# First layer of a two-layer block: half of the weight chunks get their two parts from DMAs instead of from ScalarE, VectorE and GpSimd

## The chip, the core and the metric

The kernel runs on one core of a Trainium2 chip. The metric is the device time of one execution in microseconds (us), lower is better. The core has TensorE (PE, matmuls; PEld is its weight load), VectorE (DVE), ScalarE (ACT), GpSimd (POOL), SyncE (SP, which only issues DMAs here) and 16 DMA engines. Each engine works through its own queue in order; engines wait for each other through semaphores.

## What is computed

256 tokens of width 2048 pass through two layers. The first has chunked attention (A), an RWKV-7 scan (B) and attention to a memory (C), merged under three gates; the second has causal attention, gated linear attention, a short convolution and a feed-forward part. The part of the reference that the change touches is the first layer's projections:

```python
h = rms_norm(x, norm_g)
proj = h @ w_in                       # 2048 x 16512
(aq, ak, av, az, br, bk, bv, bz, bwd, bad, cq, cz, ga, gb, gc) = jnp.split(proj, offsets, axis=-1)
ya = chunked_band_attention(aq, ak, av, a_rel_bias) * jax.nn.silu(az)
yb = rwkv7_time_mix(br, bk, bv, bwd, bad, ...) * jax.nn.silu(bz)
mk, mv = jnp.split(rms_norm(mem, mem_norm_g) @ w_mem_kv, 2, axis=-1)
yc = memory_cross_attention(cq, mk, mv) * jax.nn.silu(cz)
merged = sigmoid(ga) * (ya @ w_up_a) + sigmoid(gb) * (yb @ w_up_b) + sigmoid(gc) * (yc @ w_up_c)
return x + merged @ w_o
```

Everything is float32. The kernel gets float32 accuracy from float32r matmuls by splitting each operand into a high part (rounded to float32r) and a low part (what the rounding lost): high*high + high*low + low*high.

## The kernel before

**Weights.** All weights come from DRAM in chunks of 128 x 1024 float32 (512 KB), 963 in all. `wchunk` (L159 to L168) makes a chunk ready: SP loads it into a buffer `w` (a pool of 4), ACT rounds it into `wh` (L163, a pool of 3), and VectorE or GpSimd subtracts to give `wl` (L167, a pool of 3). A buffer is taken again when its last reader is done: `w` after the subtraction, `wh` and `wl` after the last matmul of their chunk. So chunk n can be rounded only when TensorE is done with chunk n-3.

**Products.** `gemm_B` (L170) makes 128 features x 256 tokens out of 2 chunks of 8 k tiles: for each k tile a matmul of `wh` over 512 columns (high and low activations side by side in `xg`) and one of `wl` over 256. `gemm_A` (L182) makes 256 tokens x 512 features out of 8 chunks of 2 k tiles. `evict` (L201) adds the two halves. All matmuls and transposes are recorded at L153 and L150.

**Stages.** 0 to 134 us: memory keys and values (`w_mem`, 32 chunks). 134 to 957 us: the 206 chunks of `w1A` and `w1B` that belong to `share[0] = 0.7` (set at L334). It is the share of the low parts that GpSimd makes; with the rounding of `turn*0.7` that is 161 of the 206, and VectorE makes 45. Beside these products run the memory attention, the eight pairs of RWKV heads (`rwkv_inputs`, `rwkv_inverse`, `rwkv_chain`) and the attention A. `rwkv_inverse` lets GpSimd make `lt` and `tt` (L532, L534), `rwkv_chain` lets it make `Sd` (L608). `ahead` (L677) computes 22 gates of the merge early and puts them by in DRAM (`gdram`, a GpSimd DMA). From 957 us on `share[0]` is 0: the rest of layer one, and from 1350 us the second layer, use VectorE alone for `wl`.

**Order.** Each engine's order is fixed when the program is built: a scheduler places every instruction by its own estimate of when the inputs are ready. At the chip the engines wait in that order.

Of the kernel before, what the change touches and what calls it, by code (L numbers as in the profile page):

```python
# [8 lines left out]
F32 = mybir.dt.float32  # L9
F32R = mybir.dt.float32r  # L10
BF16 = mybir.dt.bfloat16
AF = mybir.ActivationFunctionType
ALU = mybir.AluOpType
# [13 lines left out]
# columns of the per-feature parameter tile  # L27
# [10 lines left out]
# constants that depend on shapes alone  # L38
# [7 lines left out]
# masks of zeros and ones  # L46
# [43 lines left out]
def chunks(kt):  # L90
    """k tiles of 128 in chunks of 8 or a little less."""
    n = -(-kt // 8)
    base, rem = divmod(kt, n)
    o = 0
    for i in range(n):
        s = base + (i < rem)
        yield o, s
        o += s


def _body(tc, a, out):
# [9 lines left out]
    wp = pool("w", 4)  # L111
    whp = pool("wh", 3)
    wlp = pool("wl", 3)
# [42 lines left out]
    share = [0.0]  # of the low parts, those that GpSimd makes  # L156
    turn = [0]

    def wchunk(src, nel):  # L159
        w = wp.tile([128, 1024], F32, tag="w", name="w")  # L160
        nc.sync.dma_start(w[:, :nel], src)
        wh = whp.tile([128, 1024], F32R, tag="wh", name="wh")
        nc.scalar.copy(wh[:, :nel], w[:, :nel])  # L163
        wl = wlp.tile([128, 1024], F32R, tag="wl", name="wl")
        turn[0] += 1
        eng = nc.gpsimd if turn[0] * share[0] % 1.0 < share[0] else nc.vector
        eng.tensor_sub(wl[:, :nel], w[:, :nel], wh[:, :nel].bitcast(F32))  # L167
        return wh, wl  # L168

    def gemm_B(wd, act, kt=KD, m=128):  # L170
        """[features, tokens]: both halves of the sum in one bank."""
        ps = psg.tile([128, 512], F32, tag="g", name="g")
        for k0, kn in (chunks(kt) if m == 128 else [(0, kt)]):
            src = wd[128 * k0 * m:128 * (k0 + kn) * m].rearrange("(p c) -> p c", p=128)
            wh, wl = wchunk(src, kn * m)
            for j in range(kn):
                k = k0 + j
                mm(ps[:m, :], wh[:, j * m:(j + 1) * m], act[:, k, :], start=(k == 0), stop=False)
                mm(ps[:m, 256:512], wl[:, j * m:(j + 1) * m], act[:, k, 0:256], start=False, stop=(k == kt - 1))
        return ps  # L180

    def gemm_A(wd, act, kt=KD, ahead=None):  # L182
        """[tokens, 512 features] for two token tiles."""
        ps = [psg.tile([128, 512], F32, tag="g", name="g") for _ in range(2)]
        for k0 in range(0, kt, 2):
            if ahead:
                ahead(k0)
            src = wd[128 * k0 * 512:128 * (k0 + 2) * 512].rearrange("(p c) -> p c", p=128)
            wh, wl = wchunk(src, 1024)
            for j in range(2):  # L190
                k = k0 + j
                for tt in range(2):
                    hi = act[:, k, tt * 128:(tt + 1) * 128]
                    lo = act[:, k, 256 + tt * 128:256 + (tt + 1) * 128]
                    h_ = wh[:, j * 512:(j + 1) * 512]
                    l_ = wl[:, j * 512:(j + 1) * 512]
                    mm(ps[tt], hi, h_, start=(k == 0), stop=False)
                    mm(ps[tt], hi, l_, start=False, stop=False)
                    mm(ps[tt], lo, h_, start=False, stop=(k == kt - 1))
        return ps  # L200
# [13 lines left out]
    def split_to(hl, k, src, g=None):  # L214
        """hi and lo parts of src*g into hl[:, k, 0:256 | 256:512]."""
        hi = hl[:, k, 0:256]
        if g is None:
            nc.scalar.copy(hi, src)
            nc.vector.tensor_sub(hl[:, k, 256:512], src, hi.bitcast(F32))
        else:  # L220
            nc.scalar.activation(hi, src, AF.Copy, scale=g)
            nc.vector.scalar_tensor_tensor(hl[:, k, 256:512], src, g, hi.bitcast(F32), op0=ALU.mult, op1=ALU.subtract)
# [15 lines left out]
    def rsqrt(u, y):  # L238
        """u = 1/sqrt(u), with one Newton step; y is scratch of the same shape."""
# [6 lines left out]
    def stats(acc, bc=None, col=None):  # L246
        """1/rms of the tokens: one per partition in col, along the free axis in bc."""
# [28 lines left out]
    def prepare(src, acc, split, squares):  # L276
        """Loads two k tiles at a time, ahead of their products."""
# [26 lines left out]
    if True:  # L304
# [29 lines left out]
        share[0] = 0.7  # L334
        # raw branch outputs; the last part holds token-major tiles meanwhile
# [6 lines left out]
        # sums of squares per head, then 1/sqrt for q and k together  # L342
# [70 lines left out]
        def shift(dst, z, mu):  # L413
            """z [128, 257] with a zero column first; dst = z + mu*(prev - z)."""
# [15 lines left out]
        # queries and keys of four heads of A, and one of two sets of token-major tiles  # L430
# [5 lines left out]
        # block-diagonal operands: zeros stay, the diagonal blocks are rewritten  # L436
# [20 lines left out]
        def rwkv_inputs(p):  # L457
            """Products for a pair of heads, and what the chunks need of them."""
# [26 lines left out]
            # kk normalised per head  # L485
# [9 lines left out]
            # k2 = k*(1 + (a-1)*k_a)  # L495
            nc.vector.tensor_scalar(t0, av_, -1.0, P("k_a", p), op0=ALU.add, op1=ALU.mult)
            nc.vector.scalar_tensor_tensor(k, t0, 1.0, k, op0=ALU.add, op1=ALU.mult)
            # bonus weight r*k2*r_k summed per head
# [15 lines left out]
        def rwkv_inverse(p):  # L514
            """Products inside the chunks and (I - L)^-1, two chunks at a time: doubling of blocks
            in float32r, then one Newton step on the exact L."""
# [65 lines left out]
        def rwkv_chain(p):  # L582
            """The chunks in order, then group norm, affine and bonus."""
# [35 lines left out]
            # group norm per head (over the partitions of a head)  # L619
# [14 lines left out]
        def attn128(qT, kT, v_of, finish, bias, qscale, escale):  # L634
            """Two query tiles against keys 0..127 and 0..255; qT, kT [128, 256]."""
# [27 lines left out]
        def silu2(z):  # L663
            """2*silu(z), in place."""
# [12 lines left out]
        def ahead(i):  # L677
            """A gate of the merge, before its sigmoid, put by in DRAM."""
# [34 lines left out]
        # products that do not wait for the chain of the chunks, to run beside it  # L713
# [63 lines left out]
    def residual(wd, act, kt, xres, src, gname, hl):  # L777
        """xres[:, m] = src(m) + act @ w; sums of squares; split of xres*g into hl."""
# [24 lines left out]
    # ================= second layer =================  # L803
# [10 lines left out]
    # gate inputs of the decays  # L814
# [18 lines left out]
    # r gates  # L833
# [140 lines left out]
def _layout(i):  # L974
    """Layouts of the inputs; no arithmetic on them."""
    def tiles(w, n=128):
        """Column tiles of n; in each, chunks of k tiles follow one another, [128, k, n] each."""
# [69 lines left out]
```

## Time and profile before

| | |
|---|---|
| runs | 3015.86, 3016.11, 3016.77 us (median 3016.11) |
| profiled execution, span | 3013.1 us |
| median less span (start and end around the span) | 3.0 us |
| TensorE busy in the span | 2941.7 us, 98% |
| VectorE, ScalarE, GpSimd busy | 1958.8, 1448.1, 581.4 us |
| DRAM read | 514.56 MB, 172 GB/s on average |

A row of instructions gives line, engine, operation, what it writes <- what it reads, shapes and count, then busy us in all and mean ns of one, then the idle time of the engine just before and what ended it. A row of stretches gives the stretch's length, each engine's busy us (and number of instructions), then the granted TensorE clock as a share of full speed, the mean busy share of the DMA engines, and GB/s.

### The profile page before, as it was taken

What the parts mean: (1) busy time and instruction counts of PE and PEld (TensorE: products, weight loads), DVE (VectorE), ACT (ScalarE), POOL (GpSimd) and SP (SyncE); (2) the same over time, 40 slices, a digit from 0 to 9 for tenths busy, and PEclk for the clock granted to TensorE, in tenths of its full rate; (3) what the DMA queues carried; (4) which work ended last, traced back from release to release, by engine and by line L of the source; (5) the groups of instructions that cost most, each with busy time, mean ns of one, the idle gap of its engine ahead of it and who ended that gap; (6) DMA issues with size and microseconds to landing.
All of it is one profiled execution on the core that took longest, in us unless ns stands there. A gap on an engine that the chain in (4) does not pass through costs nothing.

```text
span 3013.1 us, 43980 instructions
## 1 busy us (share of the span) xinstructions
PE 2941.7 (98%) x16704; PEld 2582.1 (86%) x16704; DVE 1958.8 (65%) x3086; ACT 1448.1 (48%) x2179; POOL 581.4 (19%) x441
## 2 busy tenths in 40 slices
PE   8998999999999999999999999999999999999998
PEld 6887888887888888888888888888888888888887
DVE  6368675677764755665766766666676666666554
ACT  5454444434445645555444444445455444444443
POOL 6455555644554100000000000000000000000000
PEclk9999999999999999999999999999999999999999
DMA  7643333433435766665445555555565555556564
GB/s 253 205 142 123 129 127 121 136 98 123 133 130 180 226 189 189 202 204 171 160 161 168 183 191 191 190 189 190 188 193 186 191 191 190 189 189 186 191 190 146
DMA packets 151252, 522.42 MB, mean 173 GB/s; under 512 B 17200, under 2 KB 22320, under 8 KB 151040
## 3 DMA queue, kind: packets, MB, share of 16 engines
q1 hardware_dynamic: 148208, 512.72, 52.6%
q0 software_dynamic: 1824, 4.98, 0.4%
q8 instruction: 131, 2.15, 0.3%
q10 hardware_dynamic: 1008, 1.90, 0.2%
q14 instruction: 81, 0.66, 0.1%
HBM read 514.56 MB, written 4.98 MB: 172 GB/s over the span
## 4 chain that ended last, share of the span: by engine, by line
PE 90%; DVE 8%; POOL 1%; ACT 1%; issue 1%; DMA 0%; SPq 0%; DVEq 0%; ACTq 0%
PE g L153 83%; PE G L153 1%; PE ch L153 1%; PE D L153 1%; PE oT L153 1%; PE sc L153 1%; PE po L153 1%; PE Z L153 1%; POOL acc L293 1%; DVE kt_d L509 0%; DVE wl L167 0%; POOL sq L289 0%; DVE bt_d L508 0%; DVE tA L416 0%; DVE tt L564 0%
## 5 line engine op out<-in xcount | busy, mean ns | idle before, releaser
L153 PE MATMUL g<-xg,wh 128*128 128x512 f32 x4640 | 1641.1, 394 | 2.3 <-DVE zr L207 2.2
L163 ACT CAST wh<-w 128x1024 fp32r<-128x1024 f32 (+1 forms) x963 | 1004.1, 1043 | 1269.7 <-PE g L153 696.9
L167 DVE TENSOR_TENSOR wl<-w,wh 128x1024 fp32r<-128x1024 f32 (+1 forms) x802 | 986.6, 1231 | 740.5 <-ACT wh L163 738.6
L153 PE MATMUL g<-xg,wl 128*128 128x256 f32 x4640 | 1325.1, 286 | 4.0 <-DVE wl L167 3.8
L153 PEld LDWEIGHTS g<-xg,wh 128*128 128x128 f32 x4640 | 874.6, 189 | 179.0 <-issue 2.6
L153 PEld LDWEIGHTS g<-xg,wl 128*128 128x128 f32 x4640 | 881.8, 190 | 6.8 <-DVE wl L167 4.2
L167 POOL TENSOR_TENSOR wl<-w,wh 128x1024 fp32r<-128x1024 f32 x161 | 391.3, 2433 | 256.6 <-ACT wh L163 235.3
L153 PE MATMUL g<-yhl,wh 128*128 128x512 f32 x768 | 271.9, 393 | 3.1 <-ACT wh L163 1.8
L153 PE MATMUL g<-wh,xg 128*128 128x512 f32 x768 | 251.3, 402 | 1.7 <-DVE z L207 1.3
L153 PE MATMUL g<-act,wh 128*128 128x512 f32 x704 | 244.1, 390 | 0.0
L153 PE MATMUL g<-yhl,wl 128*128 128x256 f32 x768 | 217.7, 284 | 0.6 <-DVE wl L167 0.6
L153 PE MATMUL g<-act,wl 128*128 128x256 f32 x704 | 198.7, 282 | 0.0
L771 POOL TENSOR_TENSOR accm<-accm,z 128x256 f32<-128x256 f32 x64 | 48.0, 751 | 661.1 <-DVE z L770 661.1
L153 PEld LDWEIGHTS g<-yhl,wh 128*128 128x128 f32 x768 | 145.3, 189 | 33.8 <-ACT wh L163 3.7
L153 PEld LDWEIGHTS g<-wh,xg 128*128 128x128 f32 x768 | 143.9, 190 | 32.8 <-DVE z L207 1.6
L204 ACT COPY et<-g 128x256 f32<-128x256 f32 (+1 forms) x434 | 157.9, 364 | 10.4 <-PE g L153 7.4
L153 PEld LDWEIGHTS g<-act,wh 128*128 128x128 f32 x704 | 132.1, 188 | 27.5
L153 PE MATMUL g<-wl,xg 128*128 128x512 f32 x384 | 154.7, 403 | 0.0
L153 PEld LDWEIGHTS g<-yhl,wl 128*128 128x128 f32 x768 | 146.5, 191 | 1.2 <-DVE wl L167 1.1
L153 PEld LDWEIGHTS g<-act,wl 128*128 128x128 f32 x704 | 133.4, 189 | 0.0
L207 DVE TENSOR_TENSOR z<-g,et 128x256 f32<-128x256 f32 x216 | 90.3, 418 | 25.1 <-ACT et L204 24.8
L153 PE MATMUL g<-wh,mem_hl 128*128 128x512 f32 x256 | 83.2, 406 | 8.1 <-ACT wh L163 8.1
(349 smaller groups left out, 2960.8 us busy)
## 6 DMA issues: line engine op xcount, KB each, us to landing
w<-w2B SPq DMA_DIRECT2D x208, 512.0 KB, 3.4
w<-w1B SPq DMA_DIRECT2D x194, 512.0 KB, 3.4
w<-w_gate SPq DMA_DIRECT2D x88, 512.0 KB, 3.5
w<-w_ffup SPq DMA_DIRECT2D x88, 512.0 KB, 3.4
w<-w1A SPq DMA_DIRECT2D x64, 512.0 KB, 3.4
w<-w_down SPq DMA_DIRECT2D x64, 448.0 KB, 3.3
w<-w_mem SPq DMA_DIRECT2D x32, 512.0 KB, 4.6
w<-w_o SPq DMA_DIRECT2D x32, 512.0 KB, 4.0
```

What stands on the lines that cost most here:

```text
L153: nc.tensor.matmul(dst, lhsT=lhsT, rhs=rhs, start=start, stop=stop)
L163: nc.scalar.copy(wh[:, :nel], w[:, :nel])
L167: eng.tensor_sub(wl[:, :nel], w[:, :nel], wh[:, :nel].bitcast(F32))
L204: nc.scalar.copy(t[:m], ps[:m, 256:512])
L207: nc.vector.tensor_add(z[:m], ps[:m, 0:256], t[:m])
L293: nc.gpsimd.tensor_add(acc, acc, s)
L771: nc.gpsimd.tensor_add(accm, accm, u)
```

## The change

While `share[0]` is above zero, every second chunk (103 of 206) takes another way. GpSimd issues a DMA that casts the float32 chunk from DRAM straight into `wh`; ACT writes the negative of `wh` into `wl`; GpSimd issues a second DMA that reads the chunk from DRAM again and adds it onto `wl`. The other 103 chunks go as before, with the subtraction always on VectorE; GpSimd makes none. The pool `w` has 3 buffers instead of 4 and `wl` has 4 instead of 3, for the whole kernel. Comments that were dropped move the line numbers by about four.

```diff
-    wp = pool("w", 4)
+    wp = pool("w", 3)
     whp = pool("wh", 3)
-    wlp = pool("wl", 3)
+    wlp = pool("wl", 4)
...
     def wchunk(src, nel):
+        wh = whp.tile([128, 1024], F32R, tag="wh", name="wh")
+        wl = wlp.tile([128, 1024], F32R, tag="wl", name="wl")
+        turn[0] += 1
+        if turn[0] * share[0] % 1.0 < share[0]:
+            nc.gpsimd.dma_start(wh[:, :nel], src)
+            nc.scalar.mul(wl[:, :nel], wh[:, :nel].bitcast(F32), -1.0)
+            nc.gpsimd.dma_start(wl[:, :nel], src, accum_op=ALU.add)
+            return wh, wl
         w = wp.tile([128, 1024], F32, tag="w", name="w")
         nc.sync.dma_start(w[:, :nel], src)
-        wh = whp.tile([128, 1024], F32R, tag="wh", name="wh")
         nc.scalar.copy(wh[:, :nel], w[:, :nel])
-        wl = wlp.tile([128, 1024], F32R, tag="wl", name="wl")
-        turn[0] += 1
-        eng = nc.gpsimd if turn[0] * share[0] % 1.0 < share[0] else nc.vector
-        eng.tensor_sub(wl[:, :nel], w[:, :nel], wh[:, :nel].bitcast(F32))
+        nc.vector.tensor_sub(wl[:, :nel], w[:, :nel], wh[:, :nel].bitcast(F32))
         return wh, wl
...
-        share[0] = 0.7
+        share[0] = 0.5
```

GpSimd's queue beside the inverse and the chain of a pair of heads, in the middle of the stage (`Sd`, `lt`, `tt` are steps of those; a name's number tells buffers apart). Before:

```order
L532 TENSOR_TENSOR lt_3712<-lt_3712,con_92 128x256
L534 TENSOR_TENSOR tt_3710<-tt_3710,con_92 128x512
L608 TENSOR_SCALAR Sd_3659<-S_3644,ep_2719 128x128
L167 TENSOR_TENSOR wl_5233<-w_5229,wh_5231 128x1024
L532 TENSOR_TENSOR lt_3735<-lt_3735,con_92 128x256
L534 TENSOR_TENSOR tt_3733<-tt_3733,con_92 128x512
L167 TENSOR_TENSOR wl_5251<-w_5247,wh_5249 128x1024
L167 TENSOR_TENSOR wl_5290<-w_5286,wh_5288 128x1024
L608 TENSOR_SCALAR Sd_3676<-S_3658,ep_2719 128x128
```

Now, at the same place of the same pair:

```order
L164 DMA wh_4624<-w1B 128x1024
L612 TENSOR_SCALAR Sd_3626<-S_3611,ep_2699 128x128
L166 DMA wl_4625<-w1B 128x1024
L536 TENSOR_TENSOR lt_3679<-lt_3679,con_92 128x256
L538 TENSOR_TENSOR tt_3677<-tt_3677,con_92 128x512
L536 TENSOR_TENSOR lt_3702<-lt_3702,con_92 128x256
L538 TENSOR_TENSOR tt_3700<-tt_3700,con_92 128x512
L164 DMA wh_4677<-w1B 128x1024
L612 TENSOR_SCALAR Sd_3643<-S_3625,ep_2699 128x128
L164 DMA wh_4776<-w1B 128x1024
L166 DMA wl_4678<-w1B 128x1024
```

The subtractions are gone; casts (L164), which wait for TensorE to free a `wh`, and accumulations (L166), which wait for ACT's negative of the same chunk, stand between the steps of the pair.

GpSimd's queue near the end of the stage, where the last gates are computed ahead. Before:

```order
L167 TENSOR_TENSOR wl_8628<-w_8624,wh_8626 128x1024
L680 DMA gdram_101<-z_8570 128x256
L167 TENSOR_TENSOR wl_8678<-w_8674,wh_8676 128x1024
L608 TENSOR_SCALAR Sd_8018<-S_8000,ep_6666 128x128
L680 DMA gdram_101<-z_8620 128x256
L167 TENSOR_TENSOR wl_8700<-w_8696,wh_8698 128x1024
L680 DMA gdram_101<-z_8670 128x256
```

Now:

```order
L164 DMA wh_8404<-w1B 128x1024
L633 TENSOR_TENSOR raw_961<-raw_961,oT_7951 128x256
L164 DMA wh_8453<-w1B 128x1024
L166 DMA wl_8405<-w1B 128x1024
L684 DMA gdram_101<-z_8378 128x256
L166 DMA wl_8454<-w1B 128x1024
L164 DMA wh_8502<-w1B 128x1024
```

The last step of the last pair (L633) now has ten casts for gates behind it; before it stood behind all of these chunks.

TensorE's queue at the boundaries of chunks there (each row is one matmul). Before, a chunk of the same tile `g` follows the other:

```order
L153 MATMUL g_8673<-xg_106,wh_8676 128x512
L153 MATMUL g_8673<-xg_106,wl_8678 128x256
L153 MATMUL g_8673<-xg_106,wh_8698 128x512
L153 MATMUL g_8673<-xg_106,wl_8700 128x256
L153 MATMUL g_8673<-xg_106,wh_8698 128x512
```

Now (`wh_8404` comes by cast, `wh_8431` by SP):

```order
L153 MATMUL g_8332<-xg_106,wh_8355 128x512
L153 MATMUL g_8332<-xg_106,wl_8356 128x256
L153 MATMUL g_8381<-xg_106,wh_8404 128x512
L153 MATMUL g_8430<-xg_106,wh_8431 128x512
L153 MATMUL g_8430<-xg_106,wl_8432 128x256
```

TensorE does the first matmul of the cast chunk, leaves it, works through the SP chunk of the next tile, and comes back to the cast chunk's `wl` after that.

## Rows read from the trace of the kernel before

**Rows 1.** The page: span, and each engine's busy time.

```profile
span 3013.1 us, 43980 instructions
PE 2941.7 (98%) x16704; PEld 2582.1 (86%) x16704; DVE 1958.8 (65%) x3086; ACT 1448.1 (48%) x2179; POOL 581.4 (19%) x441
```

**Rows 2.** Stretches of the span: busy us by engine, clock, DMA share, GB/s.

```profile
134.00:180.00 46.00, 43.87 (x225) 36.41 (x223) 24.28 (x34) 25.52 (x33) 29.11 (x14) 1.00 0.52 164
180.00:900.00 720.00, 681.23 (x3991) 599.33 (x3992) 505.23 (x952) 313.38 (x482) 384.51 (x246) 0.97 0.38 125
900.00:957.00 57.00, 57.00 (x345) 50.91 (x344) 19.75 (x31) 25.52 (x38) 38.45 (x25) 1.00 0.59 184
957.00:1350.00 393.00, 389.31 (x2208) 343.26 (x2208) 255.48 (x374) 213.30 (x350) 35.15 (x53) 0.99 0.63 201
```

**Rows 3.** Stretches around a pause of TensorE, same columns as rows 2.

```profile
281.00:286.00 5.00, 1.21 (x7) 0.64 (x5) 4.91 (x7) 2.09 (x4) 2.83 (x3) 0.96 0.38 131
286.00:292.40 6.40, 4.51 (x14) 3.87 (x15) 5.93 (x12) 0.63 (x1) 2.81 (x4) 0.50 0.26 82
```

**Rows 4.** Timeline in a full-rate stretch: start us, us, engine, line, instruction.

```profile
919.62 0.39 PE L153 MATMUL g<-xg,wh 128*128 128x512 f32 x1
919.97 0.40 PE L153 MATMUL g<-xg,wh 128*128 128x512 f32 x1
920.45 1.05 ACT L163 CAST wh<-w 128x1024 fp32r<-128x1024 f32 x1 [1.73 <-issue]
921.59 2.40 POOL L167 TENSOR_TENSOR wl<-w,wh 128x1024 fp32r<-128x1024 f32 x1 [0.69 <-ACT wh L163]
```

**Rows 5.** Groups by line and form, 134 to 957 us.

```profile
L167 POOL TENSOR_TENSOR wl<-w,wh 128x1024 fp32r<-128x1024 f32 x153 | 372.1, 2435 | 232.7 <-ACT wh L163 211.4 <-issue 9.7 <-PE tra L150 7.2
L163 ACT CAST wh<-w 128x1024 fp32r<-128x1024 f32 x196 | 205.3, 1047 | 269.2 <-PE g L153 190.8 <-issue 65.4 <-POOL wl L167 5.0
L667 DVE SCALAR_TENSOR_TENSOR z<-et,z 128x256 f32<-128x256 f32 x24 | 20.7, 864 | 4.3 <-ACT et L666 4.3
L416 DVE TENSOR_TENSOR tA<-zr 128x256 f32<-128x256 f32 x25 | 19.3, 771 | 0.9 <-DVE zr L207 0.5
L242 DVE TENSOR_TENSOR t<-t,tA 128x256 f32<-128x256 f32 x8 | 10.2, 1280 | 0.1
L536 ACT CAST lmr<-lt 128x256 fp32r<-128x256 f32 x16 | 6.5, 406 | 27.6 <-POOL lt L532 27.6
L680 POOL DMA_DIRECT2D gdram<-z x20 | 11.7, 585 | 9.2 <-DVE U L598 2.9 <-DVE z L207 2.9 <-DVE mx L645 1.9
```

**Rows 6.** Groups by line and form, 1000 to 3000 us, where GpSimd makes no `wl`.

```profile
L167 DVE TENSOR_TENSOR wl<-w,wh 128x1024 fp32r<-128x1024 f32 x646 | 792.7, 1227 | 586.8 <-ACT wh L163 586.3
L242 DVE TENSOR_TENSOR osq<-osq,nw 128x256 f32<-128x256 f32 x4 | 1.7, 420 | 0.1
```

**Rows 7.** DMA issues: issuing queue, count, KB each, median us from issue to landing.

```profile
w<-w1A SPq DMA_DIRECT2D x64, 512.0 KB, 3.4
w<-wuc SPq DMA_DIRECT2D x16, 512.0 KB, 4.3
gdram<-z POOLq DMA_DIRECT2D x22, 128.0 KB, 3.9
xin<-xT POOLq DMA_DIRECT2D x16, 128.0 KB, 3.5
bias<-relb SPq DMA_DIRECT2D x8, 128.0 KB, 2.6
```

**Rows 8.** Timeline at the end of the stage: split of the raw branches for the merge.

```profile
955.38 7.17 ACT L218 CAST yhl<-raw 128x256 fp32r<-128x256 f32 x23
957.61 7.79 DVE L219 TENSOR_TENSOR yhl<-raw,yhl 128x256 fp32r<-128x256 f32 x23
```

**Rows 9.** Timeline in the second layer: a `w` buffer from subtraction to next load.

```profile
2504.29 1.23 DVE L167 TENSOR_TENSOR wl<-w,wh 128x1024 fp32r<-128x1024 f32 x1 [1.22 <-ACT wh L163]
2505.54 3.10 SPq L161 DMA_DIRECT2D w<-w_gate  x2
2505.97 1.05 ACT L163 CAST wh<-w 128x1024 fp32r<-128x1024 f32 x1 [1.46 <-issue]
2508.75 1.05 ACT L163 CAST wh<-w 128x1024 fp32r<-128x1024 f32 x1 [1.41 <-issue]
```

## The prediction

> **What bounds the kernel now.** First the page's busy times, to see which engine has no air: TensorE is busy 98% of the 3013.1 us span, VectorE 65%, ScalarE 48%, GpSimd 19% [rows 1]. Then the stretches, to see where the air is. In the stage that the change touches, 134 to 957 us, TensorE is busy 43.9 of 46, 681.2 of 720 and 57 of 57 us [rows 2]: 41 us idle in 823. The clock there is 0.97 of full over 720 us, so about 43 us run at half speed (1.2 instead of 2.4 GHz) and lose half of that, 22 us. What comes before such a spell is seen in one place: TensorE is busy 1.2 of 5.0 us while VectorE works 4.9 of the 5, then the clock is 0.50 for 6.4 us [rows 3]. Third, a timeline of a full-rate stretch: one k tile (a `wh` and a `wl` matmul) takes 0.35 us, a chunk of eight 2.8 us; ACT rounds a chunk in 1.05 us, GpSimd starts its subtraction 0.1 us later and needs 2.40 [rows 4]. From the moment TensorE frees a `wh`, then, a new chunk is ready in some 3.6 us, against the two chunks (5.6 us) that TensorE still has. That is why it can run without a gap although `wh` has only three buffers: the load itself is ahead of that loop, in `w`. So TensorE sets the end, the weight loop is hidden with 2 us to spare, and the idle time comes from the steps of the RWKV pairs.
>
> **What can be gained.** GpSimd's subtractions go: 372 us in the stage [rows 5]. They delay VectorE. The same step (L242, 128 x 256) takes 1.28 us in this stage and 0.42 where GpSimd makes no `wl` [rows 5, 6]; L416 takes 0.77 and L667 0.86 for the same amount of data. These three groups alone carry 8 x 0.86 + 25 x 0.35 + 24 x 0.44 = 26 us, and most two-operand steps of a pair are of this kind; I take 100 us for all, an estimate from these factors. The Trainium skill ("SBUF — State Buffer", Who interferes with whom) says that a VectorE instruction with two SBUF inputs and a GpSimd instruction that reads SBUF block each other for a whole instruction; the L242 pair of rows agrees. VectorE gets 103 - 45 = 58 more subtractions at 1.23 us [rows 6], 71 us. Its load thus falls by about 30 us, but the 71 us are work that can fill its pauses, and the 100 us lie in chains that TensorE waits for. The most that this can give is what TensorE loses now: 41 + 22 us, and 7 to 8 us behind 957 us, where 23 roundings and 23 subtractions of `yhl` stand in one row before the merge can start (7.2 and 7.8 us [rows 8], 3.7 idle and a clock of 0.99 over 393 us [rows 2]). These steps now start before the last ten casts. I take 30 of these 71 us: the pairs also wait for TensorE and ACT, which get no faster.
>
> **What the new way costs: its length.** A cast chunk has no `w` ahead of the loop. Cast, negative and accumulation all lie between freed `wh` and first use of `wl`. The rows of before show no cast and no accumulation, so each is bounded by plain loads. From 128 to 512 KB a load on SP's queue grows from 2.6 to 3.4 us; GpSimd's queue needs 3.5 for 128 KB [rows 7], so 4.3 for a chunk; where the DMA engines are busy 0.63 instead of 0.38 [rows 2], loads take 4.3 instead of 3.4, which would make it 5.2. The change adds 103 reads of 0.5 MB, so I take 4.6. The negative: 1.05 us, as the rounding of the same size [rows 5], and 0.6 of waiting in ACT's queue. The accumulation must read `wl` too: 512 KB more at 0.8 us per 384 KB, 1.1, so 5.7, and 0.5 for GpSimd's queue. Four hand-overs of 0.1 [rows 4]. Sum L = 4.6 + 1.05 + 0.6 + 5.7 + 0.5 + 0.4 = 12.9, say **13 us**. Lower end: 4.3 + 1.05 + 4.3 = 9.7, an accumulation at the price of a plain load and no queue. Upper end: nothing here excludes that the DMA engines convert or add at half their rate and both transfers double their moving part; with busy DMA engines 6.5 + 1 + 1 + 8 + 0.5 = 17 us.
>
> **What covers it.** I counted in TensorE's new order what stands between the matmul that frees the buffer and the first use of `wl`, at 0.35 us per k tile and 0.2 to 0.3 us per small matmul. In the first eight cast chunks (`w1A`, nothing beside them) it is two chunks and a little, 6.4 us on average. In the last sixteen it is 9.7: TensorE takes an SP chunk of the next tile first. In the 79 between, where steps of the pairs stand too, it is 13, from 8.7 to 18.8. The shortfall of one chunk overlaps with that of the next cast chunk, whose buffer is already free while TensorE waits; so half of it counts. At L = 13: 8 x 6.6 / 2 = 26; 16 x 3.3 / 2 = 26; of the 79, those below 13 lack 68 us together, half is 34. Sum **86 us**. At 9.7 it is 13 + 5 + 2 = 20, at 17 it is 42 + 58 + 161 = 261.
>
> **Queues.** GpSimd's queue holds an accumulation until ACT's negative is there, some 6 us after its cast, and behind it stand `lt`, `tt`, `Sd` and the `gdram` stores. ACT waits for `lt` already now, 27.6 us in all [rows 5]; ACT in turn stands at a negative until the cast has landed, with evictions and roundings behind it. If a third of the 64 `lt`, `tt` and `Sd` steps come 1 us later for the chain of a pair, that is 21 us: I take 20, from 0 (the scheduler put them where they fit) to 60. The 206 issues themselves take 0.585 us each [rows 5], 120 us of GpSimd instead of 372: hidden. SP loses 103 loads, ACT's count of 206 operations stays: nothing. A rule that speaks against the change: the skill's same page (SBUF: two separate sides) warns that GpSimd cannot write descriptors while VectorE holds the shared port in a two-port mode. The 0.585 us of an issue in this stage are the nearest row; at that price the rule adds nothing to the sum, and no run here shows it under accumulations.
>
> **Three `w` buffers.** In the second layer a buffer freed by the subtraction at 2504.3 is loaded from 2505.5; roundings follow at 2506.0 and 2508.7 [rows 9], 2.78 us apart. With four buffers that load is needed at the fourth, 2514.3, 4.4 to 5.4 us after it landed (3.4 to 4.3 us [rows 7]); with three at 2511.5, still 1.7 us or more ahead. Hidden, except in pile-ups and in the start, which waits for loads: 5 us, from 0 to 15. The fourth `wl` costs nothing.
>
> **Sum.** Span 3013.1 + 86 + 20 + 5 - 30 = 3094; the median of the runs lies 3.0 us over the span, so 3097, and I say **3095 us**.
>
> **Rivals.** (1) The new way is hidden and VectorE's relief shows. It decides at L of about 10 us: at 9.7 the stalls are 20 us, and if the queues cost nothing, 30 to 45 us of gain leave 2990 to 3006. For it speaks the factor of three on VectorE's steps; against it GpSimd's 3.5 us for a quarter of a chunk. The Trainium skill ("DMA: Bandwidth & Descriptors", Anatomy of one DMA) gives 2.0 us plus bytes / 436 GB/s for a GpSimd DMA, 3.2 us for a chunk; by that estimate L would be about 9 and this rival would win. The trace does not agree: the same formula gives 2.3 us for 128 KB where the row shows 3.5 [rows 7]. (2) A slow DMA path, L of 17 us or more: 3016 + 261 + 40 - 30 = 3287, and more if pauses of 4 to 5 us bring the half clock of rows 3 again and again. For it: nothing of before shows a cast or an add; against it: a plain load moves its last 384 KB in 0.8 us, so the DMA engines are far from the bound. (3) Both sides cancel, L near 10.7: stalls of about 30 us against 30, 3010 to 3022. (4) The scheduler lets the order absorb the casts elsewhere, so that the change does not do what it says to TensorE; its new order shows the covers counted above, so this is part of (1).
>
> **How the numbers follow.** Forecast, 3022 to 3200 with L from 11 to 14.5: 0.58. Rival 1: 0.20. Rival 2: 0.13. Rival 3: 0.09. A measurement of this kernel tells about 0.2%, 6 us, from no change. Faster by more than that 0.20, within it 0.09, slower 0.71. The range runs from 2988, the near end of rival 1, to 3290, where rival 2 begins; that leaves out some 0.15.
>
> **What will show it.** Right: accumulations (L166) land 5 us or more after issue; TensorE's idle time in the stage grows from 41 to over 100 us and is ended by DMAs into `wl`; the first `w1A` chunks and the last gates lose most per chunk; L242 falls from 1.28 to about 0.45 us; from 957 us on nothing changes but the `yhl` pause. Wrong: landings of 3.5 us, or a TensorE that loses its time to `lt`, `Sd` or ACT instead.

## The result, and the profile after

| | before | after |
|---|---|---|
| runs, us | 3015.86 to 3016.77 (4), median 3016.00 | 3183.21 to 3204.77 (4), median 3193.23 |
| profiled execution, span | 3013.1 | 3203.0 |
| TensorE idle in the span | 71.4 | 194.5 |
| time at the half clock | 47.8, in 9 spells | 184.3, in 37 spells |
| first load for the merge (`wuc`) issued | 946.0 | 1116.6 |

The changed kernel is slower: 1.059 times the time of before, 95% interval 1.056 to 1.062. That is 177 us more, where 79 were forecast. The direction was right and the time lies in the range, but the size was missed by more than half.

Idle time is the span less TensorE's busy time. Time at the half clock is the sum of the stretches of the trace with a granted clock of 0.50 of full (1.2 instead of 2.4 GHz), without the last one of each kernel, which lies at the end of its span. Half of it is lost where TensorE works, and nothing more where it stands, since that time is idle time already. TensorE works in 153.9 of the 184.3 us, and in 43.1 of the 47.8. So between the two profiled executions its idle time grew by 123 us and the loss by the half clock by (153.9 - 43.1) / 2 = 55 us: 178 of the 190 us that the span grew. The other 12 us are in TensorE's busy time, and no run here says what they are. (The profiled execution of after is the longest of its four; the table of all runs below goes by profiled executions and their spans.)

The page of after: span, busy times, the row of the granted clock, and two of the new transfers (KB each, median us from issue to landing).

```profile
span 3203.0 us, 43972 instructions
PE 3008.5 (94%) x16704; PEld 2619.9 (82%) x16704; DVE 1922.2 (60%) x3144; ACT 1444.3 (45%) x2176; POOL 345.3 (11%) x486
PEclk9889899899999899999999999999999999999999
wh<-w1B POOLq DMA_DIRECT2D x71, 512.0 KB, 5.3
wl<-w1B POOLq DMA_DIRECT2D x71, 512.0 KB, 5.5
```

Against [rows 1], VectorE and GpSimd are busy for less time and TensorE for more, though its matmuls are the same 16704: of the 67 us more, 55 are the half clock. The clock row is below 9 in five of the first 14 slices (to 1121 us) and in none behind them.

Stretches of after; columns as in [rows 2]. The stage now ends at 1147 us instead of 957.

```profile
100.00:200.00 100.00, 71.51 (x272) 55.45 (x271) 17.93 (x19) 26.81 (x31) 13.50 (x19) 0.85 0.62 156
200.00:1000.00 800.00, 700.64 (x3894) 607.47 (x3893) 464.86 (x1002) 305.47 (x473) 187.49 (x276) 0.93 0.62 158
1000.00:1147.00 147.00, 114.85 (x560) 95.13 (x559) 46.59 (x85) 53.04 (x84) 28.87 (x43) 0.88 0.73 179
1147.00:1545.00 398.00, 391.24 (x2221) 343.85 (x2220) 248.97 (x351) 207.02 (x330) 42.29 (x53) 1.00 0.61 200
```

TensorE is idle 28.5, 99.4 and 32.1 us in the three parts of the stage. It works for 19.5, 98.7 and 29.0 us of them at the half clock, which costs half of that: 10, 49 and 15 us. Behind 1147 us it is idle 6.8 us at full clock, against 3.7 at 0.99 in the same work of before [rows 2], and from there to the end both kernels take 2056 us: nothing is lost there, and the 7 to 8 us that the prediction saw before the merge are not won.

The timeline of the first of these pauses in after: start us, us, engine, line, instruction, and in brackets the idle time before it and what ended it.

```profile
113.31 1.06 ACT L165 ACTIVATE wl<-wh 128x1024 fp32r<-128x1024 f32 x1 [0.84 <-DMA wh<-w1A]
113.92 0.54 POOL L164 DMA_DIRECT2D wh<-w1A  x1 [4.89 <-PE g L153]
114.67 0.90 POOL L166 DMA_DIRECT2D wl<-w1A  x1 [0.21 <-issue]
119.75 1.06 ACT L165 ACTIVATE wl<-wh 128x1024 fp32r<-128x1024 f32 x1 [5.38 <-DMA wh<-w1A]
121.11 0.87 POOL L166 DMA_DIRECT2D wl<-w1A  x1 [5.54 <-ACT wl L165]
122.24 0.80 PE L153 MATMUL g<-wl,xg 128*128 128x512 f32 x1 [8.16 <-DMA wl<-w1A]
```

The chain can be read off: a cast has landed at 113.3, the negative is there at 114.4, the accumulation goes out at 114.7 and TensorE gets its `wl` at 122.2, after 8.2 us of standing. In that time the next cast chunk has gone through its cast (113.9 to 119.7) and its negative. This is the overlap that the prediction counted on.

Stretches of after around this pause, same columns as above: the pause, the work until the next one, and the spell at the half clock by itself.

```profile
113.60:122.30 8.70, 0.54 (x4) 0.10 (x2) 0.13 (x1) 1.83 (x2) 2.31 (x3) 0.71 0.75 181
122.30:135.60 13.30, 13.30 (x47) 10.60 (x48) 2.45 (x2) 2.49 (x3) 0.55 (x1) 0.80 0.49 118
117.31:127.55 10.24, 5.31 (x13) 4.15 (x14) 0.00 (x0) 1.65 (x2) 0.87 (x1) 0.50 0.66 123
```

After the pause the clock is 0.80 over 13.3 us. The `wh` matmuls behind it stand 0.43 us apart and not 0.23 for some 5 us, then at full rate. It is the pattern of [rows 3], and it comes with each of the first four pauses: the clock stands at 0.50 from 117.3, 141.2, 161.7 and 182.2 us on, for 6.8 to 10.2 us. Each of these spells begins while TensorE still stands; 3.7 to 5.5 us of each fall on its work.

Waits of after from 134 to 1150 us: who waited for what, us in total, times, longest.

```profile
POOL wl L166 <- ACT wl L165: 376.6, 73, 12.7
ACT wl L165 <- DMA wh<-w1B: 198.6, 61, 8.0
PE g L153 <- DMA wl<-w1B: 66.5, 41, 4.6
PEld g L153 <- DMA wl<-w1A: 56.1, 18, 7.9
PE g L153 <- ACT wh L170: 10.5, 9, 2.0
PE g L153 <- DVE wl L171: 7.6, 10, 1.6
```

Most of TensorE's idle time is ended by accumulations, as forecast: 126 of 160 us. GpSimd and ACT stand for the two steps ahead of them.

Groups of after by line and form, 134 to 1150 us, columns as in [rows 5]. Lines are four higher than before: L246 was L242, L420 was L416, L671 was L667, L540 was L536.

```profile
L420 DVE TENSOR_TENSOR tA<-zr 128x256 f32<-128x256 f32 x25 | 12.6, 504 | 0.3
L671 DVE SCALAR_TENSOR_TENSOR z<-et,z 128x256 f32<-128x256 f32 x24 | 10.1, 422 | 8.1 <-ACT et L670 8.0
L540 ACT CAST lmr<-lt 128x256 fp32r<-128x256 f32 x16 | 6.4, 400 | 15.9 <-POOL lt L536 15.9
L246 DVE TENSOR_TENSOR t<-t,tA 128x256 f32<-128x256 f32 x8 | 3.3, 415 | 0.0
```

VectorE's relief came as said: L242 from 1280 to 415 ns, L667 from 864 to 422, L416 from 771 to 504 [rows 5]. The Trainium skill ("SBUF — State Buffer", Who interferes with whom) has a VectorE instruction with two SBUF inputs and a GpSimd instruction that reads SBUF block each other; these rows agree. And ACT's wait for `lt` fell from 27.6 to 15.9 us, so no loss shows there from the transfers in GpSimd's queue.

The issues of the accumulations in after: duration of one in ns (least, median, most), and the time to landing.

```profile
L166 POOL DMA_DIRECT2D wl<-w1B x71: 847/872/953, 198.8 to 1145.2; - x71
L166 POOL DMA_DIRECT2D wl<-w1A x32: 852/870/914, 114.7 to 836.5; - x32
DMA to landing us min/median/max: 5.1/5.5/9.7
```

Matched chunk by chunk in the trace, the means of the 103 chains are: cast 5.65 us to its landing, 0.41 until ACT begins, negative 1.06, 0.47 until GpSimd issues, accumulation 6.21. Together **13.8 us**; the forecast had 12.9, rounded to 13.

The same matching gives what TensorE does between the issue of a cast and the first use of its `wl`, in us at the full clock: 6.0 on average in the first eight cast chunks, 11.3 in the middle (7.9 to 15.3), 10.0 in the last sixteen. By this count the shortfalls, each chain less its own cover, are 55, 205 and 69 us.

Casts also stand in GpSimd's queue. Here a cast comes out directly behind an accumulation that stood for its negative:

```profile
1017.25 0.86 POOL L166 DMA_DIRECT2D wl<-w1B  x1 [5.19 <-ACT wl L165]
1017.95 0.73 POOL L164 DMA_DIRECT2D wh<-w1B  x1
```

So it is with 21 of the 103 casts, and the accumulations before them had stood 114.7 us in all; 5 of the 16 `Sd` and 2 of the 16 `lt` stand like this too.

### The profile page after: what moved, and what is told of

It reads as the page before. It is cut to its first block, busy times and chain, and to the rows that moved or that the text cites. A ratio compares the mean times of both kernels' runs of the same rounds, so it can differ in the third digit from the quotient of the medians.

```text
span 3203.0 us, 43972 instructions
## 1 busy us (share of the span) xinstructions
PE 3008.5 (94%) x16704; PEld 2619.9 (82%) x16704; DVE 1922.2 (60%) x3144; ACT 1444.3 (45%) x2176; POOL 345.3 (11%) x486
## 3 DMA queue, kind: packets, MB, share of 16 engines
HBM read 568.56 MB, written 4.98 MB: 179 GB/s over the span
## 4 chain that ended last, share of the span: by engine, by line
PE 63%; DMA 2%; issue 2%; POOL 1%; DVE 1%; ACT 0%; DVEq 0%; POOLq 0%; SPq 0%; ACTq 0%
PE g L153 62%; DMA wl<-w1B 1%; DMA zs<-gdram 1%; DMA wh<-w1B 0%; PE glo L153 0%; POOL accm L775 0%; DVE xr L972 0%; POOL wl L166 0%; PE sc L153 0%; PE po L153 0%; PE kv L153 0%; ACT wh L170 0%; POOL wh L164 0%; POOL gdram L684 0%; PE gln L153 0%
## 5 line engine op out<-in xcount | busy, mean ns | idle before, releaser
L153 PE MATMUL g<-xg,wh 128*128 128x512 f32 x4640 | 1659.8, 398 | 19.1 <-ACT wh L170 10.5
L171 DVE TENSOR_TENSOR wl<-w,wh 128x1024 fp32r<-128x1024 f32 (+1 forms) x860 | 1054.4, 1226 | 932.5 <-ACT wh L170 931.1
L170 ACT CAST wh<-w 128x1024 fp32r<-128x1024 f32 (+1 forms) x860 | 896.0, 1042 | 1187.8 <-PE g L153 709.5
L153 PEld LDWEIGHTS g<-xg,wh 128*128 128x128 f32 x4640 | 883.3, 191 | 205.0 <-ACT wh L170 13.3
L153 PE MATMUL g<-wh,xg 128*128 128x512 f32 x768 | 272.4, 430 | 0.4 <-ACT va L322 0.4
L165 ACT ACTIVATE wl<-wh 128x1024 fp32r<-128x1024 f32 x103 | 109.1, 1059 | 270.6 <-DMA wh<-w1B 198.6
L153 PE MATMUL g<-wl,xg 128*128 128x512 f32 x384 | 170.8, 445 | 61.0 <-DMA wl<-w1A 59.8
L153 PEld LDWEIGHTS g<-wh,xg 128*128 128x128 f32 x768 | 158.8, 209 | 36.4 <-ACT va L322 0.5
L153 PEld LDWEIGHTS g<-wl,xg 128*128 128x128 f32 x384 | 81.1, 211 | 83.7 <-DMA wl<-w1A 64.7
```

The lines of the kernel that those rows point to most:

```text
L153: nc.tensor.matmul(dst, lhsT=lhsT, rhs=rhs, start=start, stop=stop)
L165: nc.scalar.mul(wl[:, :nel], wh[:, :nel].bitcast(F32), -1.0)
L171: nc.vector.tensor_sub(wl[:, :nel], w[:, :nel], wh[:, :nel].bitcast(F32))
```

## The experiments

Theory A in the texts is that of the prediction: each cast chunk has a chain of some 13 us against what TensorE has to do meanwhile, and only the shortfall costs. The rivals stand in the texts in their own words. The runs with VectorE alone, with a smaller share on GpSimd and with the pools alone start from the kernel before, the others from the changed one.

**VectorE alone, no transfer on GpSimd.**

```diff
-        share[0] = 0.7
+        share[0] = 0.0
```

> The kernel before with the GpSimd share at 0: VectorE makes all 206 low parts of the stage, no cast or accumulating DMA. It measures the relief alone. Theory A (the loss of the changed kernel comes from the long chain cast, negative, accumulation against three wh buffers, and the relief of VectorE is real): VectorE's contention goes (L242 from 1.28 to about 0.45 us), 161 subtractions of 1.23 us come on top, TensorE's idle time stays near 41 us in the stage; 2990 to 3030 us. Rival B (GpSimd and ACT waiting at the head of their queues is what costs, and taking work off GpSimd gives nothing or VectorE becomes the bound): 3030 us or more.

2981.72 us, ratio 0.989 (0.9875 to 0.9905). Better than expected: to take the subtractions from GpSimd and give all 206 to VectorE is itself a gain of 33 us. Groups and stretches of this kernel, 134 to 957 us and 100 to 905 us:

```profile
L167 DVE TENSOR_TENSOR wl<-w,wh 128x1024 fp32r<-128x1024 f32 x206 | 256.5, 1245 | 83.1 <-ACT wh L163 82.0
L416 DVE TENSOR_TENSOR tA<-zr 128x256 f32<-128x256 f32 x25 | 10.4, 416 | 0.1
L242 DVE TENSOR_TENSOR t<-t,tA 128x256 f32<-128x256 f32 x8 | 3.3, 418 | 0.0
...
100.00:200.00 100.00, 100.00 (x504) 84.28 (x503) 61.13 (x88) 50.01 (x63) 2.47 (x8) 1.00 0.53 184
200.00:905.00 705.00, 690.80 (x4131) 614.77 (x4130) 559.34 (x1080) 323.21 (x490) 84.33 (x121) 0.99 0.39 134
```

TensorE is idle 14.2 us in 805. VectorE has 161 more subtractions than before at 1.245 us, 200 us, and TensorE still waits less. So the casts cost not 177 us but 3193 - 2982 = **211 us**, against this kernel; the forecast had 86 + 20 + 5 = 111.

**A smaller share on GpSimd.**

```diff
-        share[0] = 0.7
+        share[0] = 0.25
```

> The kernel before with a GpSimd share of 0.25 of the low parts, between 0.78 (3014) and none (2982). If the contention of GpSimd's subtractions with VectorE is what the relief is made of, the time lies between, near 2990 to 3000 us; if VectorE's load in the run with none held it back, this one is faster than 2982.

2983.08 us, ratio 0.9896 (0.9881 to 0.9911): the same as none, where a time in between was expected. VectorE's steps do lie in between; this row is from 134 to 957 us:

```profile
L242 DVE TENSOR_TENSOR t<-t,tA 128x256 f32<-128x256 f32 x8 | 4.7, 587 | 0.0
```

So the time does not follow these steps in proportion. A subtraction of GpSimd also takes 2.4 us where VectorE needs 1.2, and no run separates what of the 33 us comes from the blocking and what from the longer way of a chunk.

**The pools alone.**

```diff
-    wp = pool("w", 4)
+    wp = pool("w", 3)
...
-    wlp = pool("wl", 3)
+    wlp = pool("wl", 4)
```

> The kernel before with only the pools changed (w 3 instead of 4, wl 4 instead of 3). All theories: 3016 to 3022 us; anything above 3030 would say that the smaller w pool carries a part of the loss, in the later stages too.

3019.04 us, ratio 1.0014 (1.0005 to 1.0024): 3 to 5 us, as forecast.

**The cast alone.** `wh` comes by the cast DMA, SP loads `w` as before, VectorE subtracts.

```diff
             nc.gpsimd.dma_start(wh[:, :nel], src)
-            nc.scalar.mul(wl[:, :nel], wh[:, :nel].bitcast(F32), -1.0)
-            nc.gpsimd.dma_start(wl[:, :nel], src, accum_op=ALU.add)
+            w = wp.tile([128, 1024], F32, tag="w", name="w")
+            nc.sync.dma_start(w[:, :nel], src)
+            nc.vector.tensor_sub(wl[:, :nel], w[:, :nel], wh[:, :nel].bitcast(F32))
             return wh, wl
```

> The changed kernel without the accumulation: half of the chunks get wh by the cast DMA, SP loads the same chunk into w beside it, and VectorE subtracts. Theory A: the chain from freed wh to wl is cast 5.6 + subtraction 1.2 + hand-overs 0.3 = 7.1 us instead of 13.8, under the cover of nearly all chunks; stalls under 15 us, half-clock time back near that of before; 2990 to 3030 us. Rival B (the GpSimd queue with its casts in front of the steps of the pairs): GpSimd still waits for freed buffers at each cast, so 3060 us or more.

3033.36 us, ratio 1.0065 (1.0048 to 1.0082): 52 us over VectorE alone, just above the expected range. Waits of this kernel, 134 to 1000 us:

```profile
ACT wh L171 <- DMA w<-w1B: 73.4, 19, 7.9
DVE wl L167 <- DMA wh<-w1B: 72.3, 40, 5.8
```

Now VectorE waits for casts, and ACT for SP's loads (three `w` buffers, each held until a cast has landed). The casts land after 4.6 us here.

**The accumulation alone.** SP loads, ACT rounds as before, then negative and accumulation.

```diff
-            nc.gpsimd.dma_start(wh[:, :nel], src)
+            w = wp.tile([128, 1024], F32, tag="w", name="w")
+            nc.sync.dma_start(w[:, :nel], src)
+            nc.scalar.copy(wh[:, :nel], w[:, :nel])
             nc.scalar.mul(wl[:, :nel], wh[:, :nel].bitcast(F32), -1.0)
             nc.gpsimd.dma_start(wl[:, :nel], src, accum_op=ALU.add)
```

> The changed kernel without the cast DMA: SP loads w, ACT rounds it into wh and writes the negative, and the accumulating DMA adds. Theory A: chain 1.05 + 1.06 + 0.3 + 0.5 + 6.2 = 9.1 us against a cover of 6.4 (first chunks), 13 and 9.7 us; stalls of about 20 us and 10 more by the clock; 3000 to 3060 us. Rival B: as in the changed kernel GpSimd waits for ACT at each accumulation, so half or more of the loss stays, 3100 us or more.

3041.48 us, ratio 1.0084 (1.0065 to 1.0102): 60 us over VectorE alone. The first row below is GpSimd's wait for the negative, the second TensorE's for accumulations, 134 to 1000 us:

```profile
POOL wl L168 <- ACT wl L167: 347.6, 73, 14.0
PE g L153 <- DMA wl<-w1B: 29.6, 21, 4.6
```

One half of the chain costs 52, the other 60, both in series 211, that is 99 more than the two together. This fits theory A: the two lengths one behind the other stand under one cover. It is no clean split, since each half brings waits of its own, as for SP's loads above. Both halves read as much from DRAM as the changed kernel, 568.56 MB, so the second reading as such is not what costs 211 us.

**Another cover.** Four `wh` and three `wl`, so that a cast can start a chunk earlier.

```diff
-    whp = pool("wh", 3)
-    wlp = pool("wl", 4)
+    whp = pool("wh", 4)
+    wlp = pool("wl", 3)
```

> The changed kernel with the pools wh 4 and wl 3 instead of wh 3 and wl 4: a cast may start one chunk earlier, the rest is the same. Theory A (the chain of 13.8 us from cast to landed accumulation, against the time in which TensorE uses up the other wh buffers): with one more buffer the cover counted in TensorE's new order rises from 12.3 to 13.6 us at the median and the shortfalls at 14 us halve, from 120 to 61 us; with the half clock some 90 us less than the changed kernel, 3080 to 3130 us. Theory C (GpSimd's queue in series: cast, landing 5.65, negative 1.06, accumulation issued, and only then the next cast; 8.5 us a cast chunk, 103 of them 875 us): another buffer doesn't shorten that, 3160 us or more.

3114.49 us, ratio 1.0334 (1.0316 to 1.0352), in A's range. The chain is as long as in the changed kernel (13.7 us), but the median cover, counted in TensorE's order, is 13.6 instead of 12.3 us (from the issue of the cast, in the traces, 11.9 instead of 11.0), and 79 us of the 211 are gone. If GpSimd worked off the transfers in series, a fourth `wh` would have changed little. That casts stand in its queue is not the main cost either: here 42 of them come out directly behind an accumulation, against 21.

**Half as many casts.**

```diff
-        share[0] = 0.5
+        share[0] = 0.25
```

> The changed kernel with every fourth chunk on casts (51) instead of every second (103). Theory A: each cast chunk still has to fit 13.8 us under a cover of 12 us at the median, and now no shortfall overlaps with the next one; counted in the new order 100 to 108 us of stall, with the clock 150, less 30 of VectorE's relief: 3100 to 3150 us, nearly as slow as with half. Theory C: GpSimd is busy 8.5 us for every four chunks (16 us), far from the bound: the loss all but vanishes, 2985 to 3030 us.

3060.48 us, ratio 1.0148 (1.0128 to 1.0169): under A's range and over its rival's, so both missed. With 51 casts the cost against VectorE alone is 79 us, 1.5 per cast; with 103 it is 2.0. The transfers of this kernel:

```profile
wh<-w1B POOLq DMA_DIRECT2D x35, 512.0 KB, 4.4
wl<-w1B POOLq DMA_DIRECT2D x35, 512.0 KB, 5.8
```

The cast lands after 4.4 us instead of 5.3, and the chain is 12.2 us long instead of 13.8. The accumulations are no faster than in the changed kernel; it is the casts that get slower the more is in flight (4.4 here, 4.6 with 103 casts and no accumulation, 5.3 with 103 of each). The trace of after shows it by itself: its 19 casts that no other cast or accumulation overlapped landed after 4.4 us on average, the other 84 after 5.9. And in the kernel with half as many no cast comes out directly behind an accumulation. That was in neither text.

**A longer chain.** The negative is written twice.

```diff
             nc.scalar.mul(wl[:, :nel], wh[:, :nel].bitcast(F32), -1.0)
+            nc.scalar.mul(wl[:, :nel], wh[:, :nel].bitcast(F32), -1.0)
```

> The changed kernel with the negative written twice: 1.06 us more in each chain, nothing else. Theory A: shortfalls counted in the new order at 15 instead of 14 us are 30 to 40 us more, with the clock 45 to 60: 3230 to 3260 us. Theory C: 103 times 1.06 us in series on a queue that is nearly full, about 85 to 110 us: 3270 to 3300 us.

3210.03 us, ratio 1.065 (1.0632 to 1.0668): 17 us more, less than either text. The chain is 14.8 us long, 1 us longer, but the median cover in the new order is 13.1 us instead of 12.3, and TensorE's idle time grew by 8 us only. So ACT's negative is not worked off in series with the transfers (theory C's 3270 us or more). Since the order moved too, the run does not give the price of 1 us of chain.

**No casts where nothing covers them.** The first 16 chunks of the stage go by SP.

```diff
-        if turn[0] * share[0] % 1.0 < share[0]:
+        if turn[0] > 48 and turn[0] * share[0] % 1.0 < share[0]:
```

> The changed kernel with the casts beginning at the 17th chunk of the stage: the first 16 chunks, where nothing stands between the chunks to cover a cast, all go by SP, 95 casts are left. Theory A, each stall is a local shortfall of cover and a pause brings its own half clock: what goes is the 28.5 us of idle time and half of the 30 us at half clock that 100 to 200 us hold now, 43 us: 3150, from 3135 to 3165 us. Rival B, the transfers as such are the bound and the stalls move to the next casts: 3175 us or more.

3144.02 us, ratio 1.0444 (1.0422 to 1.0466), as A said: eight casts cost 44 (by the ratios) to 49 us (by the medians). The stretch from 100 to 200 us, which had 71.51 us of TensorE and a clock of 0.85, and the first of the four copies that ACT makes of the second tile's results, when the 16 chunks are done:

```profile
100.00:200.00 100.00, 93.25 (x437) 75.76 (x436) 50.78 (x79) 43.45 (x59) 8.11 (x14) 0.97 0.61 183
155.07 0.59 ACT L320 COPY raw<-g 128x512 f32<-128x512 f32 x1 [3.85 <-PE g L153]
```

In after this copy begins at 194.12 (its row stands below). So 39 us are gone in these chunks themselves: 28 us of idle time, 10 of the half clock on work, and 1 more. The text counted half of all the 30 us at half clock, also of the part in which TensorE stood. The other 5 to 10 us lie behind, less than the runs of after differ among themselves (3183 to 3205).

**TensorE kept busy in four pauses.** 28 extra matmuls that read the cast chunk's `wh` and write a spare bank stand where TensorE waited for `wl` in four of the first eight cast chunks.

```diff
                     mm(ps[tt], hi, h_, start=(k == 0), stop=False)
+                    if share[0] > 0 and turn[0] in (34, 38, 42, 46) and j == 0 and tt == 0:
+                        fill = ps_small("fill", "o")
+                        for _ in range(28):
+                            mm(fill, hi, h_)
                     mm(ps[tt], hi, l_, start=False, stop=False)
```

> The changed kernel with 28 extra matmuls (128 x 512, 0.23 us each at full rate, 6.4 us) behind the first matmul of four of the first eight cast chunks, the four whose wl TensorE stands for 6.5 to 8.6 us; they read the cast chunk's wh and write a spare bank that nothing reads. They work where TensorE waited. Theory A, the half clock follows from the pause: the granted clock from 100 to 200 us rises from 0.85 to 0.95 or more, the chunks behind the four stalls take 2.8 us and not 5, and the first 16 chunks end 8 to 15 us earlier; the whole 3165 to 3200 us, since the order behind shifts a little too. Rival B, the half clock comes from what the DMAs or the accumulated parts do and not from the pause: the clock stays near 0.85 there, and the first 16 chunks end at the same time or up to 10 us later; the whole 3190 to 3220.

3171.39 us, ratio 1.0526 (1.0506 to 1.0547). Stretches of this kernel: the first 100 us of the new way, the former first pause, and the work behind it.

```profile
100.00:200.00 100.00, 91.19 (x388) 71.88 (x387) 18.89 (x21) 28.24 (x33) 13.53 (x19) 0.98 0.61 163
113.60:123.00 9.40, 7.71 (x33) 5.93 (x32) 0.04 (x1) 1.57 (x2) 2.31 (x3) 1.00 0.77 181
123.00:136.00 13.00, 13.00 (x57) 10.40 (x56) 2.45 (x2) 3.15 (x3) 1.97 (x3) 1.00 0.51 153
```

TensorE gets the accumulated `wl` at 122.2 us as in after, the DMA engines are as busy, and the clock is 1.00 instead of 0.80: the half clock follows from the pause and not from the transfers. What it is worth in time is another matter. The row below is the same copy of ACT in this kernel:

```profile
191.38 0.59 ACT L324 COPY raw<-g 128x512 f32<-128x512 f32 x1 [6.40 <-PE g L153]
```

And in after:

```profile
194.12 0.59 ACT L320 COPY raw<-g 128x512 f32<-128x512 f32 x1 [4.31 <-PE g L153]
```

The 16 chunks end 2.7 us earlier, not 8 to 15. The first group of four chunks took 2.3 us less (its fills begin 19.7 us apart, the pauses of after 22.0), but the chain of the third filled chunk was 17.8 us long (14.0 in after), since its negative waited 2.8 us for ACT, which was copying the first tile's results, and its accumulation landed after 8.0: TensorE came earlier and waited longer. In sum the half clock on work fell from 19.5 to 3.4 us, which gives back 8, but fills and pauses together take 34 us where the pauses took 28. The other 20 us lie behind 194 us, where the two kernels do the same work in another order, and the four runs of after differ by as much. So no difference of 20 us or less between two kernels with casts is explained in this document, but where a stretch of the trace shows it.

**VectorE alone, with four `wh`.**

```diff
-    wp = pool("w", 4)
-    whp = pool("wh", 3)
+    wp = pool("w", 3)
+    whp = pool("wh", 4)
...
-        share[0] = 0.7
+        share[0] = 0.0
```

> The kernel before with all low parts made by VectorE (as in the run that gave 2982 us) and, in the same memory, four wh and three w buffers. With no cast the rounding is 2 us ahead of TensorE already with three wh, so a fourth should give nothing there; where the pairs hold ACT up it may save some of the 51 us of idle time: 2970 to 2985 us. If w with three buffers is short of loads in pile-ups: up to 2990.

2980.70 us, ratio 0.99 (0.9885 to 0.9914): as VectorE alone. These two and the quarter on GpSimd are faster than both kernels, by 1.0 to 1.1% against before.

All runs in one table (us; idle and half clock of TensorE in the profiled execution, over the span; the last column is the span less the idle time and less half of the work at half clock):

| kernel | median | span | idle | at half clock | of it at work | the rest |
|---|---|---|---|---|---|---|
| before | 3016.00 | 3013.1 | 71.4 | 47.8 | 43.1 | 2920 |
| VectorE alone | 2981.72 | 2980.2 | 51.3 | 41.0 | 28.8 | 2914 |
| VectorE alone, four `wh` | 2980.70 | 2978.3 | 52.4 | 34.1 | 26.0 | 2913 |
| a quarter on GpSimd | 2983.08 | 2981.6 | 49.7 | 44.4 | 34.8 | 2914 |
| pools alone | 3019.04 | 3019.6 | 73.7 | 54.6 | 50.3 | 2921 |
| cast alone | 3033.36 | 3030.9 | 79.4 | 51.2 | 40.5 | 2931 |
| accumulation alone | 3041.48 | 3043.3 | 94.7 | 61.4 | 54.1 | 2922 |
| half as many casts | 3060.48 | 3071.9 | 107.0 | 102.4 | 89.5 | 2920 |
| four `wh` | 3114.49 | 3118.2 | 151.7 | 88.7 | 72.9 | 2930 |
| late start | 3144.02 | 3142.2 | 154.9 | 126.3 | 112.4 | 2931 |
| four pauses filled | 3171.39 | 3173.6 | 164.1 | 116.0 | 105.8 | 2957 |
| after | 3193.23 | 3203.0 | 194.5 | 184.3 | 153.9 | 2932 |
| two negatives | 3210.03 | 3208.5 | 202.5 | 177.5 | 137.3 | 2937 |

The last column stays within 2913 to 2937 (the filled one has 27 us of extra matmuls), so a longer span consists of idle time and half clock, but for up to 24 us that stay open. That is bookkeeping, not a cause: the filled pauses show that clock time which is won back can turn into waiting.

## Why the prediction was half right

**Right: the direction, and what brings it about.** Accumulations land after 5.5 us at the median and 6.2 on average (5.7 forecast), TensorE's idle time in the stage went from 41 to 160 us, and DMAs into `wl` end its pauses. The first cast chunks lose most per cast, (28.5 + 10) / 8 = 4.8 us, then the last sixteen, (32.1 + 15) / 16 = 2.9, and those between least, 1.6, from (99.4 - 14.2 + 49 - 9) / 79 with what VectorE alone loses there taken off.

**Right: the relief of VectorE and the pools.** 30 us were taken for the relief; the run without casts measured 33. The 5 us for three `w` buffers measured 3 to 5. What the prediction did not see is that as much was to be had without any cast.

**Wrong: the sum left out the half clock.** The prediction read it in [rows 3], and counted 22 us of it as a possible gain, but priced each new pause at its length. It stands only in rival 2, as "more if pauses of 4 to 5 us bring the half clock". The pauses of the forecast's own case are of that kind: the first eight chunks were to stand 6.6 us each. Against before, TensorE's work at the half clock grew by 111 us, a loss of 55 where the sum has nothing. In the first eight cast chunks it is most of the miss: 26 us of pauses were forecast, TensorE is idle for 28.5, and the half clock adds 10; without those casts the 16 chunks ended 39 us earlier. That a pause brings it was shown by the filled pauses. That it costs all of its 55 us was not: in the one place where it was taken away, a longer wait took back most.

**Wrong: the stalls in the middle were mis-sized.** The 79 cast chunks between were given 34 us by the rule that half of a shortfall counts, and the queues and pools 25. There TensorE is idle 99.4 us, 85 more than with VectorE alone. The rule held: the shortfalls of the trace are 55, 205 and 69 us in the three parts, and TensorE is idle for 28, 99 and 32, about half in each. What failed are its two sizes in the middle, where the prediction counted 68 us of shortfall and the trace shows 205. The chain is 13.8 us and not 13: the cast takes 5.65 us instead of 4.6, because casts get slower with what is in flight, and the accumulation 6.2 instead of 5.7, while the waits and hand-overs between take 0.9 instead of 1.5. And the cover, 13 us by the count in TensorE's order, is 11.3 from the issue of the cast. A cast that stands behind an accumulation loses cover before its issue; how much of the difference that is, no run shows. For the last sixteen 26 us were forecast, and TensorE is idle for 32.

**Half right: the queues.** 20 us were taken for steps of the pairs that stand behind transfers at the head of GpSimd's and ACT's queues. No loss shows for these steps: ACT's wait for `lt` fell to 15.9 us, and of TensorE's 160 us of idle time only 7 end on a step that is not of a weight chunk, against 37 of 41 before. But things that TensorE needs do stand there. Casts stand behind accumulations, which is part of the shorter cover above. And 18 us of TensorE's idle time end on the rounding (10.5) or the subtraction (7.6) of an SP chunk; ACT, which makes the roundings, stands at negatives for 264 us. That these chunks came late for that reason was not shown.

**The rivals.** Rival 1 needed a chain of 9.7 us; the shortest of the 103 was 10.3. The Trainium skill ("DMA: Bandwidth & Descriptors", Anatomy of one DMA) gives 2.0 us plus bytes / 436 GB/s for a DMA of GpSimd, an estimate of 3.2 us for a chunk. The rows do not agree: 5.3 us for a cast and 5.5 for an accumulation at the median; the least cast is near it, 3.5, the least accumulation is 5.1. Rival 3 needed 10.7. Rival 2's condition, a slow path of 17 us, was not met in the mean, but its remark on the half clock belonged into the forecast.

## What to carry to other kernels

When a change gives a tuned TensorE new pauses, price each pause at its length and the half clock behind it: read from the kernel's own trace how much work runs at 0.50 after a pause of that size, and add half of it, as an upper bound where the next pause is near. Do not count the part of such a spell in which TensorE stands: it is in the pause already. Price a chain of transfers at the length that it has when others of its kind are in flight, and count its cover from the issue, which can stand in a queue, and not from the moment the buffer comes free. And before work is moved from an engine that disturbs another to something new, try to give it to the one that is disturbed: here VectorE did 161 more subtractions and the kernel got 1.1% faster.

## What the runs showed of the hardware

- A cast of 512 KB from DRAM lands after 4.2 to 4.4 us with 51 casts in the stage, 4.6 with 103 and no accumulations, 4.6 to 6.5 with 95 to 103 beside as many accumulations (medians). In the changed kernel it is 4.4 us on average without and 5.9 with another cast or accumulation in flight. Plain loads of the same size on SP's queue take 3.2 to 4.7 in the medians of the same runs.
- An accumulation of the same size lands after 5.2 to 6.8 us in the medians of all these runs. In the changed kernel its issue takes GpSimd 0.87 us, that of a cast 0.56.
- GpSimd's share of simple subtractions can be worth less than nothing: with 161 of the 206 low parts on GpSimd the kernel was 1.1% slower than with none or a quarter.
- The granted clock of TensorE falls to half in the pauses of 6.1 to 8.2 us of the first cast chunks and stays there for 3.7 to 5.5 us of work; it does not where extra matmuls fill these pauses, with the same transfers in flight.
